# Layer-norm head of a hybrid decoder layer: small statistics steps and the meta tokens' scaling moved to GpSimd

## Chip, cores and metric

The kernel runs on one core of one Trainium2 chip. The metric is the device time of one execution in microseconds (us). The engines are called by the names that the profile gives them: PE (TensorE, the matmuls), PEld (TensorE's weight loads), DVE (VectorE), ACT (ScalarE), POOL (GpSimd) and SP (SyncE, which here issues the loads).

## What is computed

One decoder layer over 16 meta tokens and 1024 tokens of width 1024. Everything begins with a layer norm over each token, and this is the only part that the change touches:

```python
h = jnp.concatenate([meta, x], axis=1)      # (1, 16 + 1024, 1024)
h = layer_norm(h, in_ln_g, in_ln_b)         # (x - mean) * rsqrt(var + 1e-5) * g + b
z = h @ w_in + b_in                         # split into q, k, v, convolution input, gates
...                                         # attention branch and convolution branch, merged
h = layer_norm(ALPHA * h + mixed @ w_out, ln1_g, ln1_b)
f = (gelu(g) * u) @ ffn_w_down              # u, g: causal convolutions of h @ ffn_w_up
return layer_norm(ALPHA * h + f, ln2_g, ln2_b)[:, 16:]
```

## The kernel before

Tokens lie in tiles of 128 partitions x 1024 columns: `x0` to `x7`. The meta tokens lie twice in rows 0 to 31 of a tile `xm`; their normalised copy is written to rows 96 to 127 of the same tile. The head of the kernel turns token-major tiles into the transposed `h0` that the first product `h @ w_in` needs, in these steps:

- `stat(t, *js)`: on DVE, two BATCH_NORM_STATS2 (L395) and one BATCH_NORM_AGGREGATE (L396) for each tile give mean and variance in `mv`. Tiles are grouped by the list `tokens`; a group shares the small tiles `mv`, `t`, `r` and `m`.
- `table(t)`: on ACT, one activation (L401) gives a first value of the reciprocal square root, `r`.
- `newton(t)`: on DVE, four SCALAR_TENSOR_TENSOR (L407 to L410) make one Newton step on `r` and then `m = -mean * r`.
- `norm(t, j, on_dve)`: `x * r + m`, in two halves of 512 columns, on DVE (L428) or on ACT (L430). The result is `xn`, or the upper rows of `xm`.
- `turns(g, *ks)`: PE transposes of 128x128 blocks (L464) into PSUM tiles `ps_h0`. The group g=0 holds the meta tokens, tile 0 and tile 1; for each block of columns k the transposes of the meta tokens and of tile 0 come first (k = 0 to 3), then those of tile 1. The transposes need `ident`, a part of the tile `cols` that one DMA fills.
- `scaled(g, *ks)`: on ACT (L470), the gain and the bias of the norm, by columns, from PSUM to SBUF. `z_first(g, tiles, *ks, raw=True)`: PE matmuls of the first three output tiles (L511; later L514 with split operands).
- `scalings()`: three small DVE instructions (L413, L415, L416) that scale parts of `cols` for later use. They wait for the DMA of `cols`.

Before all that, PE runs 28 products of a tile of ones (`warm`, L538), whose results nothing uses.

The order in the head is written by hand: `in_order()` makes a list for each of DVE, ACT and PE (`dv`, `ac`, `pe`), and each instruction put in a list is ordered behind the one put there before. The rest of the kernel is ordered by ranks (`tc.cur_priority`). GpSimd has four memsets of constants, three memsets of the head (L180, L181, L204) and four subtractions far behind (L272, from 445 us on).

The lines of the head that the argument follows:

```python
stat(0, -1); table(0)
stat(1, 0);  newton(0); norm(0, -1, False)
stat(1, 1);  table(1);  scalings(); newton(1)
norm(1, 0, True); norm(1, 1, False)
turns(0, 0, 1, 2, 3)
stat(2, 2, 3, 4)
scaled(0, 0); z_first(0, (0,), 0, raw=True)
```

Of the kernel before, what the change touches and what calls it, by code (L numbers as in the profile page):

```python
# [26 lines left out]
OP = mybir.AluOpType  # L27
# [3 lines left out]
D = 1024  # L31
# [17 lines left out]
EPS = 1e-5  # L49
# [51 lines left out]
def tile_hybrid_layer(  # L101
# [3 lines left out]
    nc = tc.nc  # L105
# [15 lines left out]
    def after(ins, first):  # L121

        tc.add_manual_dep(ins.ins, first.ins.name, mybir.DependencyInfo(
            mybir.DependencyClass.NoSync, mybir.DependencyReason.SCHED_ONLY), reason="order of work")
# [243 lines left out]
    def in_order():  # L368
        done = []

        def put(ins):
            if done:
                after(ins, done[-1])
            done.append(ins)
            return ins
        return put, done

    (dv, dv_done), (ac, ac_done), (pe, pe_done) = (in_order() for _ in range(3))
    V = nc.vector
    tokens = [(-1,), (0, 1), (2, 3, 4), (5, 6, 7)]  # L380
    norms, xns = {}, {}

    def src_of(j):
        return (xt[j], P) if j >= 0 else (xm[:2 * NMETA], 2 * NMETA)

    def stat(t, *js):

        J = len(tokens[t])
        if t not in norms:
            norms[t] = [sp.tile([P, J, 2], F, name=f"mv{t}")] + [sp.tile([P, J], F, name=f"{n}{t}") for n in "trm"]  # L390
        for j in js:
            x_, n = src_of(j)
            st_ = small.tile([P, 2, 6], F, name="st")
            for i in range(2):
                dv(V.bn_stats(st_[:n, i], x_[:, i * 512:(i + 1) * 512]))  # L395
            dv(V.bn_aggr(norms[t][0][:n, tokens[t].index(j)], st_[:n].rearrange("p a b -> p (a b)")))  # L396

    def table(t):
        mv, t_, r_, m_ = norms[t]
        n = src_of(tokens[t][0])[1]  # L400
        ac(nc.scalar.activation(r_[:n], mv[:n, :, 1], AF.Abs_reciprocal_sqrt, bias=eps[:n], scale=1.0))  # L401

    def newton(t):
        n = src_of(tokens[t][0])[1]
        mv, t_, r_, m_ = (x_[:n] for x_ in norms[t])
        stt = V.scalar_tensor_tensor
        dv(stt(t_, mv[:, :, 1], EPS, r_, OP.add, OP.mult))  # L407
        dv(stt(t_, t_, -0.5, r_, OP.mult, OP.mult))
        dv(stt(r_, t_, 1.5, r_, OP.add, OP.mult))
        dv(stt(m_, mv[:, :, 0], -1.0, r_, OP.mult, OP.mult))  # L410

    def scalings():
        dv(V.tensor_scalar(qb, colA[:, 0:4], HD ** -0.5, None, OP.mult))  # L413

        dv(V.tensor_scalar(colA[:, 10:30], colA[:, 10:30], 0.5, None, OP.mult))  # L415
        dv(V.tensor_scalar(nsink, psink, -1.0, None, OP.mult))  # L416

    def norm(t, j, on_dve):
        x_, n = src_of(j)
        i = tokens[t].index(j)  # L420
        mv, t_, r_, m_ = norms[t]
        if j < 0:
            xns[j], to = xm, xm[96:]
        else:
            xns[j] = to = sp.tile([P, D], F, name="xn", tag="xn", bufs=4) if j < 4 else OB[:, (j - 4) * D:(j - 3) * D]
        for a in range(0, D, 512):
            if on_dve:
                dv(V.tensor_scalar(to[:, a:a + 512], x_[:, a:a + 512], r_[:n, i:i + 1], m_[:n, i:i + 1], OP.mult, OP.add))  # L428
            else:
                ac(nc.scalar.activation(to[:, a:a + 512], x_[:, a:a + 512], AF.Identity, bias=m_[:n, i:i + 1],  # L430
                                        scale=r_[:n, i:i + 1]))
# [21 lines left out]
    def turns(g, *ks):  # L453
        n = len(GT[g])
        c = HG[g][1] - HG[g][0]
        at = {}
        for k in ks:
            at[k] = pat.tile([P, 512], F, name="ps_h0", tag="st"[k % 2], bufs=2)
            turned[g, k] = at[k][:, n * P - c:n * P]
        for tiles in (GT[g][:2], GT[g][2:]):  # L460
            for k in ks:
                for j in tiles:
                    i = GT[g].index(j)
                    pe(nc.tensor.transpose(at[k][:, i * P:(i + 1) * P], xns[j][:, k * P:(k + 1) * P], ident))  # L464

    def scaled(g, *ks):
        a, b = HG[g]
        for k in ks:
            tm = FA[:, 1044 + 272 * k:][:, :272] if g == 0 else sp.tile([P, 384], F, name="tm", tag="tm", bufs=5)
            ac(nc.scalar.activation(tm, turned[g, k], AF.Identity, bias=b0col(k), scale=g0col(k)))  # L470
            tms[g, k] = tm

    def parts(g, *ks, hi_act=()):
        a, b = HG[g]
        for k in ks:
            tm = tms[g, k]
            if k in hi_act:
                ac(nc.scalar.copy(h0(k, 0, a, b), tm))
            else:
                dv(V.tensor_copy(h0(k, 0, a, b), tm))  # L480
            dv(V.tensor_tensor(h0(k, 1, a, b), tm, f32(h0(k, 0, a, b)), OP.subtract))
# [4 lines left out]
    def whi0(i):  # L486
        hi, lo, raw = first[i]
        ac(nc.scalar.copy(hi, raw))

    def wlo0(i):  # L490
        hi, lo, raw = first[i]
        last_split.append(dv(V.tensor_tensor(lo, raw, f32(hi), OP.subtract)))
# [7 lines left out]
    def z_first(g, tiles, *ks, raw=False):  # L500

        for i in tiles:
            a, b = span(i, g)
            if ks[0] == 0:
                sums0[i] = pat.tile([P, 512], F, name="ps_z", tag="mm", bufs=3)[:, :b - a]
        for k in ks:
            for i in tiles:
                a, b = span(i, g)
                hi, lo, w = first[i]
                if raw:  # L510
                    pe(nc.tensor.matmul(sums0[i], w[:, k], tms[g, k][:, a - HG[g][0]:], start=k == 0, stop=k == KC - 1))  # L511
                    continue
                for j, (w, hl) in enumerate(((hi, 0), (hi, 1), (lo, 0))):
                    ins = nc.tensor.matmul(sums0[i], w[:, k], h0(k, hl, a, b), start=k + j == 0,  # L514
                                           stop=k == KC - 1 and j == 2)
                    if j == 0:
                        pe(ins)
                    pe_done.append(ins)

    def lagged(g, tiles, steps):  # L520

        for t in steps:
            for l, i in enumerate(tiles):
                if 0 <= t - 2 * l < KC:
                    z_first(g, (i,), t - 2 * l)
                    if t - 2 * l == KC - 1:
                        evac(g, i)

    def evac(g, *tiles):
        for i in tiles:  # L530
            a, b = span(i, g)
            with rank(RK_EVAC):
                evacs0[i](g, a, b, sums0[i])

    tc.cur_priority = RK_START
    warm = pat.tile([P, 512], F, name="ps_w", tag="o")
    for i in range(28):
        pe(nc.tensor.matmul(warm[:, :P], ones, ones, start=True, stop=True))  # L538
    stat(0, -1)
    table(0)  # L540
    stat(1, 0)
    newton(0)
    norm(0, -1, False)
    stat(1, 1)
    table(1)
    scalings()
    newton(1)
    norm(1, 0, True)
    norm(1, 1, False)
    turns(0, 0, 1, 2, 3)  # L550
    stat(2, 2, 3, 4)
    scaled(0, 0)
    z_first(0, (0,), 0, raw=True)
    for k in range(4):
# [2 lines left out]
        z_first(0, (0,), k + 1, raw=True)  # L557
    scaled(0, 5, 6, 7)
    z_first(0, (0,), 5, 6, 7, raw=True)
    table(2)  # L560
    newton(2)
    whi0(0)
    norm(2, 2, True)
    norm(2, 3, False)
    norm(2, 4, True)
    z_first(0, (2,), 0, 1, 2, 3, 4, raw=True)
    evac(0, 0)
    wlo0(0)
# [4 lines left out]
    evac(0, 2)  # L573
    turns(1, 4, 5, 6, 7)
    evac(0, 1)
    stat(3, 5)
    wlo0(2)
    for k in range(8):
        scaled(1, k)
        parts(1, k, hi_act=(k,))  # L580
        if k == 1:
            whi0(1)
            wlo0(1)
        if k in (3, 6):
            stat(3, 6 if k == 3 else 7)
    table(3)
    newton(3)
    norm(3, 5, True)
    norm(3, 6, False)
    norm(3, 7, True)  # L590
    lagged(1, (0, 2, 1), range(8))
    turns(2, 0, 1, 2, 3)
    lagged(1, (0, 2, 1), range(8, 10))
# [159 lines left out]
    for h in range(NH):  # L753
        g, r = divmod(h, 4)
        o = ps[:2, h * 16:(h + 1) * 16]
# [30 lines left out]
    po = pat.tile([P, 512], F, name="ps_o", tag="o", bufs=1)  # L786
# [10 lines left out]
    for g in range(NKV):  # L797
        o = po[:, g * 8:g * 8 + 8]
# [21 lines left out]
    for i in range(NB):  # L820
        for g in range(NKV):
# [7 lines left out]
            for u in range(2):  # L829
# [3 lines left out]
                for h in range(2):  # L833
                    o = ps[:, h * KW:h * KW + w]
# [20 lines left out]
            for h in range(2):  # L855
                for u in range(2):
                    j = h * 2 + u
                    x = s[:, h, u, first[u]:]
# [6 lines left out]
            for n, cols_of in ((P, (0, 80)), (80, (P, 0))):  # L865
                ps = pat.tile([P, 512], F, name="ps_t", tag="t", bufs=2)
                used = [u for u in range(2) if i or n == 80 or u]
                x = slice(used[0] * 256, 512)
# [9 lines left out]
            po = pat.tile([P, 512], F, name="ps_o", tag="o", bufs=1)  # L878
            for u in range(2):
                terms = [(V[:, i - 1 + u, g], P, pts[0])] if i or u else []  # L880
                terms.append((VA[:80, 2 * i + u, g], 80, pts[1]))
                x = slice(u * 256, u * 256 + 256)
# [643 lines left out]
    for c in range(FC):  # L1526
# [8 lines left out]
        for subs in passes:  # L1535
# [3 lines left out]
            i = max(a, 2)  # L1539
# [22 lines left out]
            def tt(*x):  # L1562
                with rank(RK_CHAIN):
                    return nc.vector.tensor_tensor(*x)
# [290 lines left out]
```

## Time and profile before

| | |
|---|---|
| time, median of 3 runs | 1241.26 us (1241.05 to 1242.42) |
| time of the profiled execution | 1241.21 us |
| its span, first to last instruction | 1239.4 us |
| PE busy | 1228.1 us, 99% of the span |
| DVE busy | 1084.9 us, 88% |
| ACT busy | 579.6 us, 47% |
| POOL busy | 13.3 us, 11 instructions |
| mean granted TensorE clock | 0.998 |

The profiled execution's time is 1.8 us above its span, and 0.05 us below the median of the runs. A row of the timeline reads: start and duration in us, engine, line, operation, tile written <- tiles read, shape, count; in brackets, the idle time of the engine before it and what ended it. A row with a count merges instructions that follow each other.

### The profile page before, as it was taken

Reading aid. Unit: us, or ns where it says so; the run is one execution under the profiler, and the core shown is the slowest. Engines: PE = TensorE matmul, PEld = TensorE weight load, DVE = VectorE, ACT = ScalarE, POOL = GpSimd, SP = SyncE. Lnnn points to the kernel's source line nnn. Section 1 sums busy time; section 2 is a strip of 40 time slices with the busy share of each in tenths; the row PEclk is TensorE's granted clock in tenths of the full one; section 3 lists DMA queues with packets and bytes.
Section 4 is the critical chain, followed back from the end, with each engine's and each line's share of the span. In section 5 each row is a group of like instructions: output and inputs, shape, how many; then the busy total and the mean of one; then the engine's idle time right before and its main releaser. Section 6 shows DMA issues by size and latency. Waiting matters only on the chain.

```text
span 1239.4 us, 21709 instructions
## 1 busy us (share of the span) xinstructions
PE 1228.1 (99%) x8545; PEld 1169.1 (94%) x8545; DVE 1084.9 (88%) x1846; ACT 579.6 (47%) x1047; POOL 13.3 (1%) x11
## 2 busy tenths in 40 slices
PE   9999999999999999999999999999999999999997
PEld 8999999999999999888999999999999998888885
DVE  7899989999978798759899999998999986995697
ACT  7522335664255323344755555455454454544330
POOL 0000000000000010000000000000000000000000
PEclk9999999999999999999999999999999999999999
DMA  7296844412264655222145555544455479987722
GB/s 283 67 300 149 194 122 107 122 46 86 80 164 141 177 164 145 102 87 86 52 171 205 204 179 213 184 174 153 162 203 196 174 247 321 387 322 282 255 85 85
DMA packets 109024, 213.08 MB, mean 172 GB/s; under 512 B 31739, under 2 KB 48683, under 8 KB 108794
## 3 DMA queue, kind: packets, MB, share of 16 engines
q1 hardware_dynamic: 93002, 200.63, 49.3%
q10 hardware_dynamic: 15920, 11.07, 3.0%
q8 instruction: 67, 1.10, 0.4%
q14 instruction: 35, 0.29, 0.1%
HBM read 150.04 MB, written 62.70 MB: 172 GB/s over the span
## 4 chain that ended last, share of the span: by engine, by line
PE 96%; DVE 2%; DMA 1%; issue 0%; ACT 0%; SPq 0%; DVEq 0%
PE px L1556 14%; PE py L1556 9%; PE ps_x L1700 9%; PE ps_z L305 8%; PE ps_z L304 8%; PE ps_z L300 8%; PE ps_z L1700 7%; PE pw L1556 5%; PE pz L1556 5%; PE ps_p L300 2%; PE ps_p L304 2%; PE ps_p L305 2%; PE ps_w L305 2%; PE ps_w L304 2%; PE ps_w L300 2%; PE ps_z L514 2%
## 5 line engine op out<-in xcount | busy, mean ns | idle before, releaser
L665 DVE SCALAR_TENSOR_TENSOR FA<-cin,cols,FA 128x1026 f32<-128x1026 f32 x120 | 152.2, 1279 | 0.9
L305 PE MATMUL ps_z<-RHO,wlo 128*128 128x384 f32 (+2 forms) x324 | 104.1, 321 | 0.0
L300 PE MATMUL ps_z<-RHO,whi 128*128 128x384 f32 (+2 forms) x324 | 103.9, 321 | 0.0
L304 PE MATMUL ps_z<-RHO,whi 128*128 128x384 f32 (+2 forms) x324 | 103.9, 321 | 0.0
L305 PE MATMUL ps_z<-RHC,wlo 128*128 128x384 f32 (+2 forms) x324 | 103.8, 320 | 0.0
L304 PE MATMUL ps_z<-RHC,whi 128*128 128x384 f32 (+2 forms) x324 | 103.7, 320 | 0.0
L300 PE MATMUL ps_z<-RHC,whi 128*128 128x384 f32 (+2 forms) x324 | 103.6, 320 | 0.0
L269 ACT CAST whi<-wr 128x1024 fp32r<-128x1024 f32 x37 | 38.9, 1051 | 91.7 <-PE ps_z L304 71.6
L1366 DVE TENSOR_TENSOR RHO<-wr,RHO 128x512 fp32r<-128x512 f32 x92 | 61.9, 685 | 5.2 <-ACT RHO L1365 5.2
L1365 ACT CAST RHO<-wr 128x512 fp32r<-128x512 f32 x92 | 55.3, 619 | 23.3 <-DVE wr L1383 11.4
L300 PEld LDWEIGHTS ps_z<-RHO,whi 128*128 128x128 f32 x324 | 61.0, 188 | 0.1
L300 PEld LDWEIGHTS ps_z<-RHC,whi 128*128 128x128 f32 x324 | 61.1, 189 | 0.0
L304 PEld LDWEIGHTS ps_z<-RHO,whi 128*128 128x128 f32 x324 | 61.0, 188 | 0.0
L305 PEld LDWEIGHTS ps_z<-RHO,wlo 128*128 128x128 f32 x324 | 61.0, 188 | 0.0
L304 PEld LDWEIGHTS ps_z<-RHC,whi 128*128 128x128 f32 x324 | 61.0, 188 | 0.0
L305 PEld LDWEIGHTS ps_z<-RHC,wlo 128*128 128x128 f32 x324 | 61.0, 188 | 0.0
L1383 DVE TENSOR_TENSOR wr<-wr 128x512 f32<-128x512 f32 x88 | 60.2, 684 | 0.2
L272 DVE TENSOR_TENSOR wlo<-wr,whi 128x1024 fp32r<-128x1024 f32 x35 | 42.7, 1219 | 11.5 <-ACT whi L269 11.1
L672 ACT ACTIVATE FA<-ps_z,cols 128x384 f32<-128x384 f32 (+1 forms) x48 | 26.1, 543 | 48.4 <-PE ps_z L305 44.1
L1568 ACT COPY FA<-px 128x514 f32<-128x514 f32 (+2 forms) x23 | 13.1, 571 | 72.1 <-PE px L1556 72.0
L1365 ACT CAST ws<-wr 128x512 fp32r<-128x512 f32 x60 | 36.1, 618 | 19.3 <-DVE wr L1383 10.7
L1556 PE MATMUL px<-OA,RHO 128*128 128x258 f32 (+1 forms) x336 | 43.9, 279 | 0.0
(468 smaller groups left out, 3478.8 us busy)
## 6 DMA issues: line engine op xcount, KB each, us to landing
wr<-in_w_up_dram SPq DMA_DIRECT2D x44, 512.0 KB, 4.9
wr<-in_w_z_dram SPq DMA_DIRECT2D x30, 512.0 KB, 4.4
fd<-FA SPq DMA_DIRECT2D x44, 256.0 KB, 2.4
OB<-in_w_down_dram SPq DMA_DIRECT2D x19, 512.0 KB
qt<-qd SPq DMA_DIRECT2D x28, 256.0 KB, 3.9
sgd<-FA ACTq DMA_DIRECT2D x32, 192.0 KB, 3.0
td<-OB SPq DMA_DIRECT2D x12, 512.0 KB
sums<-fd SPq DMA_DIRECT2D x12, 512.0 KB, 7.0
```

The source lines that it names most:

```text
L269: ins = nc.scalar.copy(hi, raw)
L272: return (nc.vector if quick else nc.gpsimd).tensor_tensor(lo, raw, f32(hi), OP.subtract)
L300: ins = nc.tensor.matmul(ps, ah, bh, start=i == 0, stop=False)
L304: nc.tensor.matmul(ps, ah, bl, start=False, stop=False)
L305: last = nc.tensor.matmul(ps, al, bh, start=False, stop=i == n - 1)
L665: nc.vector.scalar_tensor_tensor(acc[c], cin[:, j:j + U], wc, acc[c], OP.mult, OP.add)
L672: nc.scalar.activation(t, ps, AF.Tanh, bias=bcol(14 + i), scale=0.5)
L1365: nc.scalar.copy(hi, src)
L1366: ins = nc.vector.tensor_tensor(lo, src, f32(hi), OP.subtract)
L1383: ins = nc.vector.tensor_tensor(*x)
L1556: ins = nc.tensor.matmul(o, x[:, ks], bmat(sub, q, hl, k), start=first and k + j == 0, stop=k == 3 and j == 2, skip_group_check=not first)
L1700: nc.tensor.matmul(banks[i], l[:, ts], r[:, ws], start=first and a and x + k == 0, stop=z and x == len(ops) - 1 and k == 2, skip_group_che ...
```

## The change

The two first token tiles no longer share a group: `tokens` becomes `[(-1,), (0,), (1,), (2, 3, 4), (5, 6, 7)]`, so that every later group's number rises by one. A fourth ordered list, `po`, is made for GpSimd. The Newton step of the meta tokens (group 0) and of tile 0 (group 1) is made on GpSimd, in seven instructions each. The meta tokens' `norm` is made on GpSimd too, as two instructions over 32x1024 elements, a multiplication by `r` in place and an addition of `m` into rows 96 to 127; `r` and `m` are read as operands repeated along the columns. Tile 0 is normalised on ACT and tile 1 on DVE, where it was the other way round. `scalings()` stands behind the statistics of the tiles 2 to 4. The warm-up products are 25 where they were 28.

```diff
-    (dv, dv_done), (ac, ac_done), (pe, pe_done) = (in_order() for _ in range(3))
+    (dv, dv_done), (ac, ac_done), (pe, pe_done), (po, po_done) = (in_order() for _ in range(4))
-    tokens = [(-1,), (0, 1), (2, 3, 4), (5, 6, 7)]
+    tokens = [(-1,), (0,), (1,), (2, 3, 4), (5, 6, 7)]
...
     def newton(t):
...
+        if t < 2:
+            tt, ts = nc.gpsimd.tensor_tensor, nc.gpsimd.tensor_scalar
+            po(ts(t_, mv[:, :, 1], EPS, -0.5, OP.add, OP.mult))
+            po(ts(mv[:, :, 0], mv[:, :, 0], -1.0, None, OP.mult))
+            po(tt(m_, r_, r_, OP.mult))
+            po(tt(t_, t_, m_, OP.mult))
+            po(ts(t_, t_, 1.5, None, OP.add))
+            po(tt(r_, r_, t_, OP.mult))
+            po(tt(m_, mv[:, :, 0], r_, OP.mult))
+            return
...
+        if j < 0:
+            for o, op, x in ((x_, OP.mult, r_), (to, OP.add, m_)):
+                po(nc.gpsimd.tensor_tensor(o, x_, x[:n].to_broadcast([n, D]), op))
+            return
...
-    for i in range(28):
+    for i in range(25):
...
     stat(0, -1)
     table(0)
+    newton(0)
     stat(1, 0)
-    newton(0)
+    table(1)
+    newton(1)
     norm(0, -1, False)
-    stat(1, 1)
-    table(1)
+    stat(2, 1)
+    table(2)
+    norm(1, 0, False)
+    newton(2)
+    norm(2, 1, True)
+    turns(0, 0, 1, 2, 3)
+    stat(3, 2, 3, 4)
     scalings()
-    newton(1)
-    norm(1, 0, True)
-    norm(1, 1, False)
-    turns(0, 0, 1, 2, 3)
-    stat(2, 2, 3, 4)
```

The rest of the diff renumbers groups 2 and 3 to 3 and 4.

More of the change, by code (lines that the diff above doesn't have):

```diff
@@ L559, in tile_hybrid_layer @@
     z_first(0, (0,), 5, 6, 7, raw=True)
-    table(2)
-    newton(2)
+    table(3)
+    newton(3)
     whi0(0)
-    norm(2, 2, True)
-    norm(2, 3, False)
-    norm(2, 4, True)
+    norm(3, 2, True)
+    norm(3, 3, False)
+    norm(3, 4, True)
     z_first(0, (2,), 0, 1, 2, 3, 4, raw=True)
@@ L575, in tile_hybrid_layer @@
     evac(0, 1)
-    stat(3, 5)
+    stat(4, 5)
     wlo0(2)
@@ L584, in tile_hybrid_layer @@
         if k in (3, 6):
[L585 to L590, printed above, removed]
+            stat(4, 6 if k == 3 else 7)
+    table(4)
+    newton(4)
+    norm(4, 5, True)
+    norm(4, 6, False)
+    norm(4, 7, True)
     lagged(1, (0, 2, 1), range(8))
```

## The prediction

> **What bounds the kernel now.** I read the page first, then the chain of waits of the first 60 us in order of time, the list of what PE waited for, and the busy time by stretches. The page says that PE is the bound, and that the chain which ended last is nearly all PE.
>
> ```profile
> span 1239.4 us, 21709 instructions
> PE 1228.1 (99%) x8545; PEld 1169.1 (94%) x8545; DVE 1084.9 (88%) x1846; ACT 579.6 (47%) x1047; POOL 13.3 (1%) x11
> PE 96%; DVE 2%; DMA 1%; issue 0%; ACT 0%; SPq 0%; DVEq 0%
> ...
> PE ps_h L464 <- DVE xn L428: 0.8, 1, 0.8
> PE ps_s L836 <- DMA qt<-qd: 0.4, 1, 0.4
> PE pw L1556 <- DVE OA L1241: 0.4, 1, 0.4
> PE ps_z L511 <- ACT FA L470: 0.3, 1, 0.3
> ...
> 20.00:40.00 20.00, 20.00 (x123) 19.12 (x122) 14.97 (x31) 15.28 (x29) 0.00 (x0) 1.00 0.37 111
> 120.00:142.00 22.00, 21.61 (x140) 21.29 (x140) 20.52 (x22) 7.65 (x13) 0.00 (x0) 1.00 0.82 178
> ```
>
> Once PE has begun its products it hardly waits: behind the head the list has two waits of 0.4 us. So the head counts by one number, the moment at which PE begins to work without gaps; what that moment loses, the end loses, less at most the 0.8 us of those two waits, and I take none of that back, because the chains that end in them hang on PE's own earlier results. The chain of the head:
>
> ```profile
> 2.58 6.65 DMA cols<-in_cols_dram
> 9.25 0.17 DVE qb L413
> ...
> 10.06 0.17 DVE m L410
> 10.26 0.56 DVE xn L428
> 10.86 1.11 PE ps_h L464 x8
> 11.99 0.59 ACT FA L470
> 12.62 0.73 PE ps_z L511 x2
> ```
>
> DVE waits for `cols` until 9.23 (2.58 + 6.65) only because `scalings` stands ahead of the Newton step; then come Newton, the first half of tile 0, eight transposes, the first `scaled` and the first product at 12.62. The transposes of `xm` and tile 0 run from 10.86; from there to the first product are 12.62 - 10.86 = 1.76 us. I call the time at which both operands of these transposes are there T: it was about 10.8.
>
> **The change part by part.** What the new order could gain: without `scalings` and the shared group, tile 0 needs only its own statistics.
>
> ```profile
> 4.83 0.20 DVE L396 BATCH_NORM_AGGREGATE mv<-st 32x2 f32<-32x12 f32 x1
> 5.06 0.29 ACT L401 ACTIVATE r<-mv,eps 32x1 f32<-32x1 f32 x1 [2.83 <-DVE mv L396]
> 6.51 0.21 DVE L396 BATCH_NORM_AGGREGATE mv<-st 128x2 f32<-128x12 f32 x1
> 6.78 0.15 DVE L408 SCALAR_TENSOR_TENSOR t<-t,r 32x1 f32<-32x1 f32 x1
> 6.96 0.15 DVE L409 SCALAR_TENSOR_TENSOR r<-t,r 32x1 f32<-32x1 f32 x1
> 7.22 1.27 DVE L395 BATCH_NORM_STATS2 st<-x 128x6 f32<-128x512 f32 x2
> 7.33 1.52 ACT L430 ACTIVATE xm<-xm,m,r 32x512 f32<-32x512 f32 x2 [1.98 <-DVE m L410]
> 8.53 0.21 DVE L396 BATCH_NORM_AGGREGATE mv<-st 128x2 f32<-128x12 f32 x1
> ```
>
> Tile 0's variance is there at 6.72, its `r` from ACT about 0.3 us later, at 7.05. Tile 1's statistics can start when DVE leaves tile 0, at 6.7 in place of 7.22, and end about 8.2; its `r` comes at 8.5. With both Newton steps at no cost, ACT would make the first half of tile 0 (half of 1.52, 0.76) from 8.5 to 9.3, and `cols` is there at 9.23: T could be 9.35, a gain of 1.5 us. This is the best that the head can give, and only if the meta tokens are also there by then. They stood at 8.85 (7.33 + 1.52) and bounded nothing.
>
> Now the meta tokens go through GpSimd, in the order: seven small steps for the meta tokens, seven for tile 0, and only then the two 32x1024 instructions. The trace of before has this engine doing a two-operand elementwise instruction of 1024 columns four times, and memsets:
>
> ```profile
> 0.24 0.10 POOL L1844 MEMSET const-float32-0.0<- 128x1 f32 x1 [0.24 <-issue]
> 0.73 0.94 POOL L180 MEMSET xm<- 32x1024 f32 x1 [0.29 <-POOLq L1844]
> 1.73 0.57 POOL L204 MEMSET tab<- 128x572 f32 x1
> 456.29 3.24 POOL L272 TENSOR_TENSOR RW<-OB,RW 128x1024 fp32r<-128x1024 f32 x1 [8.30 <-DMA OB<-sgd]
> 488.34 2.41 POOL L272 TENSOR_TENSOR wlo<-wr,whi 128x1024 fp32r<-128x1024 f32 x1 [28.81 <-ACT whi L269]
> 504.06 2.49 POOL L272 TENSOR_TENSOR wlo<-wr,whi 128x1024 fp32r<-128x1024 f32 x1 [13.32 <-ACT whi L269]
> ```
>
> That 32 partitions cost less than 128 these rows deny: the memset over 32 partitions took 0.94 us for 1024 columns (0.92 ns each), that over 128 took 0.57 for 572 (1.0 ns). The columns count. So each of the two scalings costs 2.45 us (the mean of 2.41 and 2.49), bounded below by the memset's 0.94, were a repeated operand as cheap as none, and above by 3.24. I take 2.45, since form and width are the same; the two are 4.9 us, and with a 0.1 us step between them 5.0.
>
> The small steps have no row. Below, a 128x1 memset is 0.10 us, with no operand to read. Above, DVE's chained small steps start 0.18 apart (6.78 to 6.96), and GpSimd's wide instruction takes twice DVE's 1.22 us for the same subtraction:
>
> ```profile
> 443.81 1.22 DVE L272 TENSOR_TENSOR wlo<-wr,whi 128x1024 fp32r<-128x1024 f32 x1
> ```
>
> so 0.36. I take 0.25, nearer to the chained row than to the memset, which neither reads nor waits. Then the meta tokens' seven steps run from 5.08 (variance at 5.03; ACT's `r` at 5.35 is no hindrance to the third step) to 6.83, and tile 0's seven from 6.83 to 8.58, `r` at 7.05 again being early enough. With 0.10 they end at 7.05 + 5 x 0.10 = 7.55; with 0.36 at 5.08 + 14 x 0.36 = 10.1.
>
> T is then 8.58 + 5.0 = 13.6, where it was about 10.85: **2.75 us later**. Bounds: 7.55 + 4.9 = 12.45 (1.6 later) with the cheap small steps; 10.1 + 5.0 = 15.1 (4.25 later) with the dear ones. Everything that leaves the other engines buys nothing against that: DVE loses Newton's four steps for the meta tokens (from 6.64 to 7.29), ACT loses 1.52 us and gains one 0.3 us table look-up; both then wait.
>
> `scalings`: three DVE steps that start at 9.25 and end 0.25 us of DVE time later, moved behind the statistics of tiles 2 to 4. DVE idles there anyway, until ACT's `r`:
>
> ```profile
> 16.88 0.16 DVE L407 SCALAR_TENSOR_TENSOR t<-mv,r 128x3 f32<-128x3 f32 x1 [0.53 <-ACT r L401]
> 17.68 1.52 ACT L430 ACTIVATE xn<-x,m,r 128x512 f32<-128x512 f32 x2
> 18.58 1.00 DVE L428 TENSOR_SCALAR OB<-x,r,m 128x512 f32<-128x512 f32 x2
> 19.89 1.04 PE L464 MATMUL ps_h<-cols,xn 128*128 128x128 f32 x8
> ```
>
> So it costs nothing; with that 0.53 us gone it would cost 0.25 in a stretch where the norms of tiles 2 to 4 end (19.58) near PE's use of them (19.89). What is late next if DVE is held up: this same pair. As PE itself is 2.75 us later there (22.6), DVE may be as late, and I count zero. No DMA is issued by a moved step, and SP's queue is passed by none.
>
> The three warm-up products fewer are on no path, since PE waits anyway: zero, with a rival below.
>
> GpSimd and DVE can also block each other. DVE's L1149 shows it: its median is 418 ns, but one that was issued during GpSimd's instruction at 488.34 lasted until that was over (490.75).
>
> ```profile
> L1149 DVE SCALAR_TENSOR_TENSOR RHO<-OB,RHO x14: 411/418/1964, 427.7 to 503.1; 128x256 fp32r<-128x256 f32 x14
> 488.72 0.43 DVE L1141 SCALAR_TENSOR_TENSOR OB<-OB,ps_p 128x258 f32<-128x258 f32 x1 [0.35 <-PE ps_p L298]
> 489.06 1.96 DVE L1149 SCALAR_TENSOR_TENSOR RHO<-OB,RHO 128x256 fp32r<-128x256 f32 x1
> ```
>
> L1149 reads two tiles of SBUF; L1141, with one operand in PSUM, went through in 0.43. Tile 1's Newton steps on DVE also read two SBUF tiles. They are due at 8.55, GpSimd's first scaling starts at 8.58: if GpSimd wins, each step may stand behind one scaling, and Newton ends after the second, at about 13.6 + 0.6 = 14.2, tile 1's first half at 14.75. Its transposes are due 0.9 us behind T (eight transposes, 1.11 less the overlap), at 14.5. So this costs 0 to 0.3 us; I take 0. [...]
>
> The sum, against the profiled execution's own 1241.21: 1241.21 + 2.75 = 1243.96, say 1244.0. The runs' median is 0.05 above that execution, which changes nothing.
>
> **The rivals.** First, the other side: a repeated operand costs GpSimd nothing, and each scaling runs at the memset's 0.94 us. Then with the small steps at 0.25 T is 8.58 + 1.9 = 10.5, with those at 0.10 it is 9.45: 0.3 to 1.4 us sooner than before, 1239.8 to 1240.9. It decides from a scaling of (10.85 - 8.58) / 2 = 1.1 us downward. For it speaks that the second operand is one value in a partition; against it the four rows of 2.41 us and more. 0.12.
>
> Second, PE's clock. In the first 5 us the warm-up ran at about half pace:
>
> ```profile
> 1.00:6.00 5.00, 4.92 (x23) 4.92 (x24) 2.41 (x10) 1.52 (x3) 2.20 (x3) 1.00 0.71 249
> 6.00:9.00 3.00, 3.00 (x29) 3.00 (x29) 2.55 (x9) 1.65 (x3) 0.00 (x0) 1.00 0.89 321
> ```
>
> 23 records in 5 us against 29 in 3 us. With 25 products in place of 28, six records fewer at 3/29 us each, PE ends its warm-up about 0.6 us sooner, near 8.9, and then stands idle until T, 4.7 us. If an idle stretch of that length brings the slow pace back, the next products run at half pace for as long as it took to leave it, at worst the 4.9 us from 1.08 to about 6: 2.4 us lost, less where ACT sets the pace. I price it at 1.2 to 2.4 more: 1245.2 to 1246.4. Nothing in the trace has PE idle for so long between products. [...] I give it 0.2 as the case of the median run.
>
> Third, the two engines block each other in earnest: both scalings at 3.24, and tile 1 behind them. T is 8.58 + 6.5 = 15.1, and tile 1's half another 0.3 late: 4.5 us, 1245.7. The row of 3.24 speaks for it, the small number of DVE instructions at that time against it. 0.1.
>
> That the order on GpSimd is not the written one, so that the meta tokens' scalings run before tile 0's Newton step, would move the load to tile 0: its steps would begin at 6.83 + 5.0 = 11.8, end at 13.6, and ACT's half at 14.3. That is 3.5 later, 1244.7, inside the range. 0.03.
>
> **How the numbers follow.** The forecast has 0.55, the rivals 0.12, 0.2, 0.1 and 0.03. A measurement here tells about 0.2% (2.5 us) from no change. The forecast reaches from 1.6 to 4.25 later, so it lies on both sides of that: of its 0.55 I put 0.28 above 2.5 us and 0.27 below. Slower is then 0.28 + 0.2 + 0.1 + 0.03 = 0.61, the same is 0.27 + 0.12 = 0.39, and faster by 2.5 us has no case, since the head can give 1.5 at most; I leave 0.01 of the second number for it. The forecast's own range is 1242.8 to 1245.5. The 8-in-10 range takes in the clock's case up to 1246.9 and half of the fast rival, down to 1241.2.
>
> **What would show each step.** In the changed kernel's timeline: fourteen small POOL instructions between 5 and 9 us, 0.25 apart; two POOL TENSOR_TENSOR `xm` of 32x1024 at about 8.6 and 11.1, 2.45 each; the first transpose of `xm` at 13.6 with a PE wait of some 4 us that POOL ends; the first L511 at 15.4; then no wait of PE that was not there before. The scalings at 1 us each would make the sum wrong, and so would small steps far from 0.25; a slower pace of L464 and L511 behind the wait would be the clock's case; L428 of tile 1 or L407 lasting 2 us would be the blocking.

## The result, and the profile after

The changed kernel takes 1243.59 us (median of 13 runs, 1243.04 to 1246.04); the kernel before took 1240.89 us in the same comparison (13 runs, 1240.01 to 1242.42). The ratio is 1.0024, 95% interval 1.0016 to 1.0032: 2.7 us slower. 1244.0 was predicted, within 1241.2 to 1246.9. The profiled execution of the changed kernel took 1244.15 us, its span is 1242.4 us, 3.0 more than that of before (1239.4).

The page of the changed kernel, the span, the engines and the chain that ended last:

```profile
span 1242.4 us, 21708 instructions
PE 1229.4 (99%) x8539; PEld 1169.8 (94%) x8539; DVE 1086.8 (87%) x1842; ACT 578.3 (47%) x1046; POOL 19.7 (2%) x27
PE 96%; DVE 2%; DMA 1%; ACT 1%; POOL 1%; issue 0%; DVEq 0%; SPq 0%; ACTq 0%; POOLq 0%
```

POOL is new in the chain. The chain of the head, in order of time (start, duration, engine, tile and line; rows of `issue` between the rows shown, 0.17 us at most, are left out here and in the later chains; from the norm on, the code of before sits 14 to 16 lines higher, so L464 is now L478, L511 is L525 and L428 is L442):

```profile
8.48 0.19 POOL m L414
8.67 1.85 POOL xm L438
10.58 1.90 POOL xm L438
12.53 1.22 PE ps_h L478 x9
13.78 0.59 ACT FA L484
14.41 1.28 PE ps_z L525 x2
15.69 0.64 PE ps_h L478 x3
16.33 0.91 PE ps_z L525 x2
...
19.21 4.01 PE ps_z L525 x18
```

The same block of 18 products in the chain of before:

```profile
16.04 4.01 PE ps_z L511 x18
```

So the first product is 14.41 - 12.62 = 1.79 us late, but the block of 18 is 19.21 - 16.04 = 3.17 us late: on the way from one to the other a further 1.38 us were lost. The second term is not a wait. The first pair of products took 0.73 us in the chain of before and takes 1.28 here, the second took 0.46 and takes 0.91, and the three transposes between them take 0.64 in place of 0.33.

The stretches below are cut at the steps of the granted clock and, where the clock did not change, in the same length of 3.41 us. The columns of the changed kernel's rows are the length, PE's busy time with its number of instructions, the granted clock, DMA share and GB/s:

```profile
7.00:10.41 3.41, 2.73 (x24) 1.00 1.01 406
10.41:13.83 3.42, 1.30 (x12) 1.00 1.03 419
13.83:17.24 3.41, 3.18 (x12) 0.50 1.03 412
```

The granted clock was 0.50 for 3.41 us, from 13.83 to 17.24. The steps of the clock in this trace, at 7.00, 13.83, 17.24 and 1239.21 us, lie 6.83, 3.41 and 1221.97 us apart, 2, 1 and 358 times 3.4133; the two in the trace of before, at 5.95 and 1234.75, lie 1228.80 us apart, 360 times that. PE was busy for 1.30 us of one stretch of this length, and for the next it got half the clock, though it was busy for 3.18 us of that one. The kernel before has a thin stretch too, less thin (length, PE, PEld, DVE, ACT, POOL, clock), and kept its clock:

```profile
9.36:12.78 3.42, 2.24 (x18) 1.77 (x18) 2.51 (x11) 2.31 (x4) 0.00 (x0) 1.00 1.01 412
```

What PE waited for, in the changed kernel:

```profile
PE ps_h L478 <- POOL xm L438: 2.8, 1, 2.8
...
PE pw L1572 <- DVE OA L1257: 0.4, 1, 0.4
...
PE px L1572 <- ACT OB L1584: 0.2, 1, 0.2
```

The wait of 0.4 us for `qt` near 142 us is gone and a new one of 0.2 stands far behind; the 3.17 us of the head become 3.0 at the end.

**Theory:** the meta tokens come late from GpSimd (1.8 us), and the wait that this makes for PE costs its clock (1.2 to 1.4 us more). **Rivals:** the small steps or the new order do the harm; the slow pace has another cause than PE's idle time, or is made up for later; the column scalings carry part of it.

### The profile page after: what moved, and what is told of

Same layout as the page of the kernel before. It is cut to its first block, busy times and chain, and to the rows that moved or that the text cites. A ratio compares the mean times of both kernels' runs of the same rounds, so it can differ in the third digit from the quotient of the medians.

```text
span 1242.4 us, 21708 instructions
## 1 busy us (share of the span) xinstructions
PE 1229.4 (99%) x8539; PEld 1169.8 (94%) x8539; DVE 1086.8 (87%) x1842; ACT 578.3 (47%) x1046; POOL 19.7 (2%) x27
## 4 chain that ended last, share of the span: by engine, by line
PE 96%; DVE 2%; DMA 1%; ACT 1%; POOL 1%; issue 0%; DVEq 0%; SPq 0%; ACTq 0%; POOLq 0%
PE px L1572 14%; PE py L1572 9%; PE ps_x L1716 9%; PE ps_z L304 8%; PE ps_z L305 8%; PE ps_z L300 8%; PE ps_z L1716 7%; PE pw L1572 5%; PE pz L1572 5%; PE ps_p L300 2%; PE ps_p L304 2%; PE ps_p L305 2%; PE ps_w L300 2%; PE ps_w L305 2%; PE ps_w L304 2%; PE ps_z L528 2%
```

## Experiments

**Keep PE busy.** The changed kernel with more warm-up products:

```diff
-    for i in range(25):
+    for i in range(38):
```

> The changed kernel with 38 warm-up products in place of 25, so that PE is busy until about 12.3 us; nothing else differs. Theory: the loss of 2.7 us is two terms, a first product that is 1.8 us late because the meta tokens come late from GpSimd, and 1.4 us of half pace because PE stood idle from 9.7 to 12.5 us. Then the first L525 stays at 14.4 us, no granted clock of 0.50 shows behind it, and the time falls by 1.2 to 1.4 us to about 1242.3. Rival: the idle time has nothing to do with the pace, or the pace costs nothing in the end: 1243.6 as before.

1242.26 us against 1240.62 of before, ratio 1.0014 (1.0005 to 1.0023). Its chain, its waits and two stretches (columns as for the kernel before):

```profile
12.41 1.22 PE ps_h L478 x9
...
14.28 0.72 PE ps_z L525 x2
...
17.70 4.01 PE ps_z L525 x18
...
PE ps_h L478 <- POOL xm L438: 0.3, 1, 0.3
...
9.30:12.71 3.41, 3.11 (x29) 2.92 (x28) 3.30 (x4) 0.79 (x2) 2.97 (x2) 1.00 1.03 422
12.71:16.10 3.39, 3.05 (x23) 2.56 (x22) 3.32 (x8) 2.45 (x5) 0.00 (x0) 1.00 1.03 416
```

The meta tokens come as late as before, the first product starts where it did, but the block of 18 is 17.70 - 16.04 = 1.66 us late in place of 3.17, and 1.64 us remain of the loss of 2.70. Useless products at the right time bought 1.06 us. The intervals of the two ratios overlap, so the medians alone would not settle this; the traces do: the granted clock stays at 1.00 behind the wait, and from the first product to the block of 18 it is 17.70 - 14.28 = 3.42 us, as in the kernel before (16.04 - 12.62), where the changed kernel takes 4.80.

**Take the meta tokens off GpSimd**, and leave all other parts of the change:

```diff
-        if j < 0:
-            for o, op, x in ((x_, OP.mult, r_), (to, OP.add, m_)):
-                po(nc.gpsimd.tensor_tensor(o, x_, x[:n].to_broadcast([n, D]), op))
-            return
```

> The changed kernel, but the meta tokens' scaling stands on ACT again (two halves, as before the change); all the Newton steps that the change put on GpSimd stay there. Theory: the two wide GpSimd instructions are the whole harm. The meta tokens are then ready on ACT at 8.5 us, tile 0's first half at 9.6, the first product comes at about 11.4 (12.62 before the change), the clock stays up, and the time is 1.2 us below that of before, 1239.7. Rival: the small steps on GpSimd or the new order cost as well: 1240.9 or more.

1239.32 us against 1240.62, ratio 0.999 (0.9982 to 0.9999): 1.3 us faster than before.

```profile
9.65 1.11 PE ps_h L474 x8
...
11.41 0.72 PE ps_z L521 x2
...
14.83 4.01 PE ps_z L521 x18
```

First product 11.41, as expected, and the block of 18 is 1.21 us earlier than before. The fourteen small GpSimd steps do no harm; two wide instructions are the whole of it. This version beats both kernels.

**Make PE idle without GpSimd.** The kernel before with fewer warm-up products:

```diff
-    for i in range(28):
+    for i in range(16):
```

> The kernel before the change with 16 warm-up products in place of 28: PE ends them near 7 us and is then idle but for one transpose until 10.9. No GpSimd work is added. Theory of the clock: the granted clock is 0.50 for some 3 to 6 us behind the wait, the first product moves little (at most 0.6 us later, its transposes being slower) and the time rises by 1.5 to 2.7 us to 1242.4 to 1243.6. Rival (idle time of PE in the head is free): 1240.9, no change.

1242.65 us against 1240.62, ratio 1.0014 (1.0006 to 1.0023). Stretches cut at the clock's steps (columns as for the kernel before):

```profile
7.17:10.58 3.41, 0.98 (x8) 0.63 (x6) 2.96 (x13) 2.46 (x4) 0.00 (x0) 1.00 1.02 414
10.58:14.00 3.42, 3.39 (x13) 2.88 (x14) 3.35 (x8) 2.34 (x6) 0.00 (x0) 0.50 1.03 422
...
16.98 4.01 PE ps_z L511 x18
```

Taking away work whose result nobody reads made the kernel 2.0 us slower. The clock's fall needs no GpSimd. Not all of the 2.0 us is seen in the head: in the trace the block of 18 is 16.98 - 16.04 = 0.94 us late and the span 1.4 us longer (1240.8 against 1239.4), of which 0.5 is a longer wait for `qt` (0.9 us, 0.4 before); whether that wait has to do with the clock is not shown.

**The new order with nothing on GpSimd**, Newton steps on DVE and the meta tokens on ACT:

```diff
-        if t < 2:
+        if t < 0:
...
-        if j < 0:
-            for o, op, x in ((x_, OP.mult, r_), (to, OP.add, m_)):
-                po(nc.gpsimd.tensor_tensor(o, x_, x[:n].to_broadcast([n, D]), op))
-            return
```

> The changed kernel's order and grouping with none of the added GpSimd work: the Newton steps of all groups on DVE, the meta tokens' scaling on ACT. Theory: DVE now waits for ACT's table look-up before each Newton step and does its statistics of tile 1 only from 8.7 us, so tile 1's first half is ready at about 11.9 and the first product comes at 12.7, as before the change: 1240.9, 0.5 us to either side. Beside the kernel with only the meta scaling on ACT this shows what the small steps on GpSimd buy (1.2 us). Rival: the new order alone gives the gain and GpSimd gives none of it: 1239.7 here too.

1242.23 us against 1240.62, ratio 1.001 (1.0001 to 1.0019): neither 1240.9 nor 1239.7. I had followed tile 1 on DVE and not tile 0 on ACT, whose norm stands behind tile 1's table look-up in ACT's list; and I had left out the clock.

```profile
10.15 0.03 ACT r L401
10.36 0.81 ACT xn L440
11.21 1.11 PE ps_h L474 x8
...
12.97 1.28 PE ps_z L521 x2
...
8.80:12.22 3.42, 1.36 (x12) 1.15 (x11) 2.88 (x10) 2.36 (x4) 0.00 (x0) 1.00 1.02 417
```

The first product at 12.97 is only 0.35 us late, and takes 1.28 as at half pace. From execution to execution the time went with the mean granted clock: 1240.59 and 1240.80 us at 0.999, 1241.82 to 1243.27 at 0.996 to 0.997. Then the same with 35 warm-up products:

> The changed order with nothing on GpSimd, and 35 warm-up products in place of 25. With 25 it took 1242.2, first product at 13.0, and the granted clock fell at 12.2 us after PE had been idle from 9 to 11.2. Theory: the late tile 0 (its norm stands behind tile 1's table look-up on ACT) costs 0.35 us and the clock the other 1.2; with PE kept busy the time is 1240.8 to 1241.0. Rival: the clock's fall is no more than a sign, and the order itself costs: 1242.2.

1240.83 us against 1240.34, ratio 1.0004 (0.9995 to 1.0013), as the theory has it.

```profile
12.91 0.73 PE ps_z L521 x2
```

The same first product, at the full pace. What the small steps on GpSimd buy in this order is then 12.91 - 11.41 = 1.5 us of head: with Newton on DVE, DVE waits twice for ACT's table value (0.36 us each) before it goes on to the next tile's statistics, and tile 0's norm on ACT comes later with them.

**GpSimd's order.** In the changed kernel the meta tokens' norm ahead of tile 0's Newton step:

```diff
-    newton(1)
     norm(0, -1, False)
+    newton(1)
```

> The changed kernel with one pair of lines exchanged, so that on GpSimd the meta tokens' two wide instructions stand ahead of tile 0's seven small ones. Theory (GpSimd's queue in its order is the path to the first transposes): the wide ones run from 6.9 to 10.7, the small ones to 12.6, ACT's first half of tile 0 is ready at 13.4, the first product comes at 15.2 (14.4 in the changed kernel), and with the half pace behind the wait the time is about 1244.3, 3.7 above before. Rival: only the wide instructions' end counts; then the meta tokens, ready at 10.7, take the first product to 12.6 and the time back to 1240.6.

1245.08 us (4 runs) against 1240.38, ratio 1.0038 (1.0024 to 1.0051).

```profile
8.63 1.90 POOL xm L438
10.61 0.19 POOL t L408
...
12.81 0.82 ACT xn L444
13.68 2.61 PE ps_h L478 x11
16.31 1.27 PE ps_z L525 x2
```

GpSimd's queue is the path: `xm` is there at 10.5, and tile 0 waits for what stands behind it. The transposes begin at 13.68 (13.4 expected). The clock had fallen before them (0.79 on the mean from 11 to 12 us, 0.50 from 12 to 18), so they too are slow, eleven in 2.61 us where nine took 1.22 in the changed kernel, and the loss is 4.7 us in place of 3.7.

**Half the columns at a time.** The changed kernel with the meta tokens' scaling cut in two:

```diff
-            for o, op, x in ((x_, OP.mult, r_), (to, OP.add, m_)):
-                po(nc.gpsimd.tensor_tensor(o, x_, x[:n].to_broadcast([n, D]), op))
+            for a in (0, 512):
+                s = slice(a, a + 512)
+                for o, op, x in ((x_, OP.mult, r_), (to, OP.add, m_)):
+                    po(nc.gpsimd.tensor_tensor(o[:, s], x_[:, s], x[:n].to_broadcast([n, 512]), op))
```

> The changed kernel, but the meta tokens' scaling on GpSimd is cut in two halves of 512 columns, each multiplied and added before the next; the work is the same, in four instructions. Theory (what counts is when the first 512 columns are there, and a GpSimd instruction costs by its columns): each takes 0.95 us, the first half is there at 10.6, PE waits only about 1 us, the granted clock stays at 1.00, and the first product comes at 12.5, or at 13.0 if DVE's steps of tile 1 are held up by GpSimd four times in place of two; time 1240.6 to 1241.1. Rival (a GpSimd instruction costs a fixed time whatever its width, or the whole tile counts): 12.5 or later for the first half, 14.4 for the first product and 1243.3 or more.

1241.90 us against 1240.38, ratio 1.0009 (1.0 to 1.0018): 0.8 us above the theory's range and 1.4 below the rival's. The first product came at 13.33.

```profile
8.48 1.03 POOL L440 TENSOR_TENSOR xm<-xm,r 32x512 f32<-32x512 f32 x1
...
10.68 2.52 DVE L444 TENSOR_SCALAR xn<-x,r,m 128x512 f32<-128x512 f32 x2
...
7.53:10.94 3.41, 1.08 (x10) 0.89 (x9) 2.87 (x7) 1.81 (x3) 3.01 (x7) 1.00 1.03 419
```

The first half is there at 10.7, as expected, and a half costs 1.03 us. But the clock fell at 10.94, to 0.50 for 3.41 us. To tell the clock from what DVE's longer steps beside GpSimd cost (here 2.52 us for two halves of tile 1), the same with 32 warm-up products:

> The kernel whose meta tokens are scaled on GpSimd in two halves, with 32 warm-up products in place of 25; nothing else. That kernel came out at 1241.9 where 1240.6 to 1241.1 was expected; in its profile the granted clock fell to 0.50 at 10.9 us, and single runs lay between 1240.9 and 1243.6. Theory (the clock is the difference): PE's warm-up now ends about 1.5 us later, close to the first transposes, the clock stays, and the time is 1241.0, with a spread under 1 us. Rival (the four GpSimd instructions cost that time themselves, by holding up DVE's steps of tile 1): 1241.9 as before.

1240.84 us against 1240.34, ratio 1.0003 (0.9995 to 1.0012), spread 1.1 us where less than 1 was expected. In its trace the granted clock is 1.00 from 9 to 17 us. So the clock was the difference; the 0.5 us that are left are tile 1's:

```profile
10.68 1.35 DVE xn L444
12.08 0.34 PE ps_h L480
...
13.07 0.73 PE ps_z L527 x2
```

DVE's first half of tile 1 starts at 10.68 and takes 1.35 us, where such a half took 0.56 in the chain of before: in the kernel with 25 products, where tile 1's halves start at 10.68 too, GpSimd's third instruction of 512 columns runs from 10.70 for 1.03 us. Here the half ends at 12.03. Two of tile 1's Newton steps (8.61 and 9.76) had taken 0.93 and 0.90 us, the other two 0.17.

**The column scalings alone**, in the kernel before, moved behind the statistics of the tiles 2 to 4:

```diff
-    scalings()
     newton(1)
...
     stat(2, 2, 3, 4)
+    scalings()
```

> The kernel before with one part of the change alone: the three column scalings behind the statistics of the tiles 2 to 4. Theory: they cost only what the DMA of the columns comes later than ACT's table value, 0.3 us in the profile of before; the first product comes at 12.3 to 12.6 and the time moves by 0 to -0.3 us, 1240.3 to 1240.6, which 5 rounds can hardly tell from none. Rival: they carry a good part of the 1.3 us that the changed kernel gains once the meta tokens are on ACT: 1239.9 or less.

1240.45 us against 1240.38, ratio 0.9999 (0.999 to 1.0009): no change; the first product came at 12.51 in place of 12.62.

**What a wide GpSimd instruction costs by its form**, the kernel before with ten of them on scratch tiles:

```diff
...
+    for n_, full, po_ in 2 * ((32, 1, pr), (32, 0, pr), (P, 1, pr), (P, 0, pr), (P, 1, pq)):
+        b_ = xt[1][:n_] if full else norms[1][3][:n_, 0:1].to_broadcast([n_, D])
+        ins = nc.gpsimd.tensor_tensor(po_[:n_], xt[0][:n_], b_, OP.mult)
...
```

> The kernel before with ten GpSimd multiplications of 1024 columns added behind the statistics of tile 1, on scratch tiles that nothing reads; only their durations count. Twice this order: 32 rows with a full second operand, 32 rows with one value repeated along the columns, 128 rows full, 128 rows repeated, 128 rows full written as fp32r. The changed kernel's wide instructions took 1.88 us where the four rows of before (128 rows, full, fp32r) said 2.45. Three causes would differ: the repeated operand (then 1.9 for the repeated kinds, 2.4 for the full ones), the 32 rows (1.9 for both kinds of 32 rows, 2.4 for those of 128), or the fp32r output (2.4 for the last kind alone). I hold the repeated operand for the likeliest, one stream of columns less to read.

The second five of the ten in the timeline (`x,x` full operand, `x,m` repeated):

```profile
21.11 2.34 POOL L556 TENSOR_TENSOR pr<-x,x 32x1024 f32<-32x1024 f32 x1
23.53 1.90 POOL L556 TENSOR_TENSOR pr<-x,m 32x1024 f32<-32x1024 f32 x1
25.50 2.35 POOL L556 TENSOR_TENSOR pr<-x,x 128x1024 f32<-128x1024 f32 x1
27.93 1.96 POOL L556 TENSOR_TENSOR pr<-x,m 128x1024 f32<-128x1024 f32 x1
29.85 2.52 POOL L556 TENSOR_TENSOR pq<-x,x 128x1024 fp32r<-128x1024 f32 x1
```

The repeated operand is the cause: 1.90 and 1.96 against 2.34 and 2.35. The number of rows changes 0.01 and 0.06 us; the fp32r output took 2.52 here and 2.35 in the first five, the f32 output of as many rows 2.35 and 2.43. Of the first five, one is off: the repeated kind with 32 rows took 2.18 from 12.18 on, when a TENSOR_SCALAR of DVE was under way since 12.07. The kernel as a whole took 1255.24 us in a single run, its head held up by the ten.

## Why the prediction was right, step by step

The total was right by luck as much as by the path: two misses of opposite sign nearly met. With the clock held up by 38 warm-up products the same path costs 1.64 us, 1.1 less than the 2.75 forecast and near the low end of its bounds (1.6); the clock, which the sum left out, made up the rest.

**The path** was right: GpSimd's chain of fourteen small steps and two wide ones sets the start of the transposes, PE waits for it, and what the head loses stays to the end but for 0.2 us.

**The small steps** were right. 0.25 us was taken between a memset's 0.10 and 0.36. They start 0.17 to 0.30 apart, and the last one ends at 8.67, where 8.58 was predicted:

```profile
6.92 0.19 POOL L408 TENSOR_SCALAR t<-mv 128x1 f32<-128x1 f32 x1
7.17 0.23 POOL L409 TENSOR_SCALAR mv<-mv 128x1 f32<-128x1 f32 x1
...
8.62 1.88 POOL L438 TENSOR_TENSOR xm<-xm,r 32x1024 f32<-32x1024 f32 x1
10.58 1.89 POOL L438 TENSOR_TENSOR xm<-xm,m 32x1024 f32<-32x1024 f32 x1
```

**The wide steps** are the term that was mis-sized: 2.45 us each from the rows of the same name and width, 1.88 measured. The rows had a full second operand, this one a repeated value. That was named as a rival's mechanism, at the extreme of 0.94, and given no middle; 1.88 is about three fifths of the way from the memset to the full operand. T came out at 12.5, not 13.6, and the first product 1.8 us late, not 2.75.

**The clock** is the step that failed in its weight: it stood as a rival at 0.2, priced at 1.2 to 2.4 us, and it is part of the result, at 1.38 us in the profiled execution and 1.06 between the medians with 25 and with 38 warm-up products. The traces show steps that lie whole multiples of 3.41 us apart, at a phase that differs by execution (a step at 5.95 us in the profile of before, at 7.00 in that of after; ahead of this first recorded step the clock's column reads 1.00, though a warm-up product of before took 421 ns in the median from 1 to 5 us and 275 ns in the median of all 56). The clock was 0.50 in the stretch that followed 3.41 us with PE busy for 0.98, 1.08, 1.30 or 1.36 us, and stayed at 1.00 after 2.24. The chance of 0.2 was the author's estimate and is shown by no run; its case was an idle time of 4.7 us. Here a wait of 2.8 us came before the fall in the changed kernel, and one of 2.1 us in the kernel with nothing on GpSimd; with PE kept busy in that time (38 and 35 products) the clock stayed at 1.00. The wait itself was forecast too long: PE's warm-up was put to end near 8.9, though the row of the warm-up in before ends at 9.90 (1.08 + 8.82) and 0.6 sooner is 9.3; it ended at 9.73, and T was 12.53.

**The two engines blocking each other** happened and cost next to nothing, as forecast. In the changed kernel one Newton step (L419, L409 before) lasted until 10.52 and one half of tile 1 until 12.77, and GpSimd's two scalings beside them ended at 10.50 and 12.47:

```profile
8.77 1.75 DVE L419 SCALAR_TENSOR_TENSOR r<-t,r 128x1 f32<-128x1 f32 x1
...
10.76 2.01 DVE L442 TENSOR_SCALAR xn<-x,r,m 128x512 f32<-128x512 f32 x1
```

Such a TENSOR_SCALAR takes 0.54 us in the kernel before (the mean of its group). It reads one tensor from SBUF where the L1149 of before reads two, so the rows of before did not say that it would last longer; this trace shows it. Tile 1's first half is there at 12.77, before its transposes are due behind T: hidden here, and 0.5 us of path in the kernel with the halves, where T is 10.7. None of tile 1's halves ran between the two scalings: the second scaling starts at 10.58, 0.08 us behind the end of the first, and the half at 10.76.

**The scalings** at nothing: shown. **The three warm-up products fewer** were costed at nothing beside the clock's rival; how much of the clock's fall they bring by themselves was not run. The rival of the other side (meta tokens in time, 0.3 to 1.4 us faster) is what the kernel with the meta tokens on ACT did by another way.

## What to carry to other kernels

Before moving work to an idle engine, set its queue out in order and its price by a row of the same form, operands included: here the idle engine's whole queue decided who waited (2.7 us lost in one order, 4.7 in the other), and a repeated operand made 1.88 us of the 2.45 that were reckoned. When a wait of PE appears or grows in a short head, ask what its clock does in the next microseconds; here a few useless products that fill the wait bought back 1.06 of the 2.70 us that were lost. Then take the change apart: here its good parts (groups apart, small steps on GpSimd) were worth 1.3 us, and the meta tokens' two wide instructions cost more than that.

## What the runs showed of the hardware that was not expected

- The granted TensorE clock was 0.50 for 3.41 to 3.42 us after a stretch of that length in which PE was busy for 0.98 to 1.36 us (29 to 40%, four kernels); after 2.24 us (66%, the kernel before) it stayed at 1.00. At the end of the changed kernel it stayed at 1.00 after 1.69 us (50%, from 1232.39 to 1235.80) and was 0.50 from 1239.21 on, after 3.41 us without work for PE. In the head of the kernel with GpSimd's order exchanged it was 0.50 for 6.8 us, from about 11.6 to 18.4: worked out from PE's waits, PE was busy for about 0.8 us of the 3.41 us ahead of that, and for about 1.3 us of the first half of it.
- A GpSimd TENSOR_TENSOR of 1024 columns took 2.34 to 2.52 us with two full operands in the kernel with the ten, 1.9 to 2.0 with one value repeated (2.18 once, beside DVE), for 32 rows as for 128; of 512 columns with a repeated value 1.03 to 1.10.
- DVE's TENSOR_SCALAR between SBUF tiles, with one tensor operand, took 2.01 us in place of 0.54 in the changed kernel, from 10.76 to 12.77, while GpSimd's second scaling ran from 10.58 to 12.47. In the kernel with GpSimd's order exchanged two of GpSimd's small steps, at 11.33 and 11.84, took 0.42 and 0.39 us in place of 0.19 and 0.21 while DVE's two halves of tile 1 ran from 11.16 to 12.16; that they waited for DVE was not shown.
